# A hybrid decoder step on one core: the input projection by Strassen pairs, its forms made ahead of the recurrence, the pooling behind it

## The chip, the core and the metric

The kernel runs on one core of a Trainium2 chip. The core has a matmul engine (TensorE, PE in the profile, with PEld for its weight loads), VectorE (DVE), ScalarE (ACT), GpSimd (POOL) and an engine that issues DMAs (SyncE, SP). Each engine runs its own list of instructions in order and waits on semaphores for the others. The metric is the device time of one execution in microseconds (us); smaller is better.

## What is computed

One step of a one-layer decoder for 512 prompt tokens and 64 sample tokens, 576 columns in all, of 1024 features in float32:

```python
h = rms_norm(x, g_mix)
u, zq, zf, zi, zg, ga, gb = split(h @ w_in)            # 512 512 512 512 512 1024 1024 columns
pooled = multiscale_pool([state_pool; u]) - u          # windows 2, 4, 8, 16, one per group of 128
pool_out = einsum('btgc,gcd->btgd', pooled, w_pool_mix) * pool_scale
fg = lb + (1 - lb) * sigmoid(zf)
o, s_new = hgrn2_recurrence(silu(zq), 1 - fg, zi, log(fg), state)   # 4 heads, in chunks
o = o * rsqrt(mean(o * o) + eps) * hgrn_norm * silu(zg)
x = x + (sigmoid(ga) * (pool_out @ w_pool_up) + sigmoid(gb) * (o @ w_hgrn_up)) @ w_out
x = x + (silu(h2 @ w_ffn_gate) * (h2 @ w_ffn_up)) @ w_ffn_down      # h2 = rms_norm(x)
x = x + sigmoid(h3 @ w_ple_gate) * (p @ w_ple_proj)                 # h3 = rms_norm(x)
y = rms_norm(x, g_final)
```

The last 15 rows of u and the states of the recurrence are outputs too.

## The kernel before

Activations lie transposed: 128 features on the partitions, 576 tokens along the free dimension, in two halves of 288 (`H0`, `H1`). float32 products are made of two parts: every operand is split into a rounded high part and the rest, and a product is three matmuls, high by high, high by low and low by high.

A **unit** is 128 output features. In plain form (`mm`, L141) it takes 8 steps of 128 input features, 3 matmuls and 2 halves: 48 matmuls of 288 columns. Its weights come by one DMA of 512 KB into `raw`, and `split` makes `whi` on ACT (L78) and `wlo` on DVE (L79); with `src` given, `split_dma` has ACT write the negated weights (L87) and POOL issue a DMA that adds the weights to them in memory (L88). The list `seq` gives the order of the units, and `next_unit` loads and splits some units ahead.

A **Strassen pair** makes two units at once. Units by halves of tokens are a 2 x 2 product of blocks, and the Winograd form of Strassen's identity needs 7 block products in place of 8. Each is 4 steps x 3 matmuls = 12 matmuls of 288 columns, so a pair takes 84. On the side of the activations it needs seven **forms** per step: B11, B21 and B22 are the normed inputs, S1, S2, U3 and U4 are sums of them, all split in two parts (`form`, L811). On the side of the weights it needs sums of the two units' halves, each split again (A, B, C, D). Before the change the branch gates ga and gb and most of the feed-forward run by pairs (`pair`), with products software-pipelined over two sets of four PSUM banks; the first 20 units of the input projection run plain.

The stage around the change, in program order:

- Three units start with the loading of x, while the norm's sums are made. POOL adds some squares (L257). `rms` gives `rn`, the reciprocal norm (L285 on ACT, L286 on DVE), and `scaled` (L361) multiplies it into a unit's result.
- The units of `seq`: 0 to 3 are the pooling's input u, 8 to 11 f of the four heads, then by heads 16 (g), 4 (q), 12 (v), and so on. In PSUM `mm0` has four places of two banks, later `mm1` has two and `aux` four single banks.
- Pooling: `pool_in` (L385) scales u into a tile with the old state in front, `pool_vec` (L397) adds shifted copies and takes u off, `pool_mix` (L416) is the matmul per group. They are spread between the units.
- Recurrence per head: `forget` and `logf` (gate and its logarithm), `decays` (sums over chunks by scans and the factors by small POOL instructions, L443 to L478), `q_in` and `q_vec` (scaled q and k), `part1` (transposes and scores), `part2` (state updates, the tiny matmuls of L597), `part3` (output), `part4` (norm and gate), `part5` (split into `oh`, `ol`). Head h's parts stand between the units of head h + 1.
- Behind the heads come four pooled up units (`up_unit`, from `pho`), the last head's parts beside them, then four from the heads' outputs `oho`. The forms of the normed input are made beside these four (L815 to L822), then the pairs of ga and gb begin.

A scheduler of the language sets each engine's list from the program order and its own estimate of readiness; on the engine the list is fixed.

Of the kernel before, what the change touches and what calls it, by code (L numbers as in the profile page):

```python
# [28 lines left out]
def trunk(ctx: ExitStack, tc: tile.TileContext, a, o):  # L29
# [84 lines left out]
    state = {"raw": 0, "split": 0, "use": 0, "lim": out0, "pe": None}  # L114
    raws, splits = {}, {}

    def ahead(n_raw, n_split):
# [237 lines left out]
    def unit_mm(xs, pz=None):  # L355
        u = next_unit()
        pz = pz or ps_mm()
        mm(pz, u, xs)
        return pz

    def scaled(out, pz, rn):  # L361
        tt(out=v2(out), in0=pz[:, :, 0:HT], in1=v2(rn), op=MULT)  # L362
# [404 lines left out]

# [603 lines left out]
```

## Time and profile before

| what | value |
|---|---|
| median of 3 runs | 833.74 us (833.62 to 833.76) |
| profiled execution, first to last instruction | 831.3 us |
| PE busy | 820.8 us, 99% |
| DVE, ACT, POOL busy | 605.9, 505.0, 112.2 us |
| norm's matmuls end, fourth unit starts | 27.4 us |
| first pooled up unit starts | 182.3 us |
| first pair of ga starts | 237.1 us |

The profiled execution has no time of its own beside its span; the 2.4 us up to the median lie before the first and behind the last instruction. A row of instructions has its start and duration or, grouped, count, busy time and mean, then the idle time of the engine just before it with what ended it. L12 is line 12 of the kernel. Matmuls are pipelined: the spacing of their starts is their price, not their duration.

### The profile page before, as it was taken

Reading aid. Unit: us, or ns where it says so; the run is one execution under the profiler, and the core shown is the slowest. Engines: PE = TensorE matmul, PEld = TensorE weight load, DVE = VectorE, ACT = ScalarE, POOL = GpSimd, SP = SyncE. Lnnn points to the kernel's source line nnn. Section 1 sums busy time; section 2 is a strip of 40 time slices with the busy share of each in tenths; the row PEclk is TensorE's granted clock in tenths of the full one; section 3 lists DMA queues with packets and bytes.
Section 4 is the critical chain, followed back from the end, with each engine's and each line's share of the span. In section 5 each row is a group of like instructions: output and inputs, shape, how many; then the busy total and the mean of one; then the engine's idle time right before and its main releaser. Section 6 shows DMA issues by size and latency. Waiting matters only on the chain.

```text
span 831.3 us, 15196 instructions
## 1 busy us (share of the span) xinstructions
PE 820.8 (99%) x6092; PEld 807.0 (97%) x6092; DVE 605.9 (73%) x1008; ACT 505.0 (61%) x829; POOL 112.2 (13%) x194
## 2 busy tenths in 40 slices
PE   8999999999999999999999999999999999999996
PEld 7999999999999999999999999999999999999996
DVE  7977777764887776547978778777787767558846
ACT  7356436557777665446667767666676666645534
POOL 6204120000111110000111221112211121000000
PEclk9999999999999999999999999999999999999999
DMA  7421231222747674246866687657876668462103
GB/s 261 143 81 51 76 106 62 97 102 80 191 101 184 166 171 141 76 108 146 185 133 143 142 215 182 151 133 176 193 178 162 130 154 202 125 170 92 62 2 114
DMA packets 39046, 111.95 MB, mean 135 GB/s; under 512 B 4928, under 2 KB 9280, under 8 KB 38976
## 3 DMA queue, kind: packets, MB, share of 16 engines
q1 hardware_dynamic: 24288, 74.51, 26.8%
q0 software_dynamic: 12528, 33.30, 23.8%
q10 hardware_dynamic: 2160, 3.19, 1.0%
q8 instruction: 47, 0.77, 0.4%
q14 instruction: 23, 0.19, 0.1%
HBM read 105.98 MB, written 5.00 MB: 133 GB/s over the span
## 4 chain that ended last, share of the span: by engine, by line
PE 91%; DVE 3%; DMA 2%; ACT 2%; POOL 1%; issue 1%; SPq 0%; DVEq 0%
PE bb L877 7%; PE bb L876 7%; PE bb L878 7%; PE mm L155 5%; PE mm L153 5%; PE mm L157 5%; PE ba L878 4%; PE ba L877 4%; PE ba L876 4%; PE bd L878 2%; PE bd L877 2%; PE bd L876 2%; PE bc L877 2%; PE bc L876 2%; PE bc L878 2%; PE ba L157 2%
## 5 line engine op out<-in xcount | busy, mean ns | idle before, releaser
L78 ACT CAST whi<-raw 128x1024 fp32r<-128x1024 f32 (+2 forms) x50 | 46.8, 940 | 71.2 <-PE mm L155 36.6
L153 PE MATMUL mm<-hh,whi 128*128 128x288 f32 x320 | 70.6, 301 | 1.4 <-DVE ta L362 0.9
L155 PE MATMUL mm<-hl,whi 128*128 128x288 f32 x320 | 70.0, 298 | 0.4 <-DVE hl L246 0.3
L157 PE MATMUL mm<-hh,wlo 128*128 128x288 f32 x320 | 68.8, 296 | 0.0
L79 DVE TENSOR_TENSOR wlo<-raw,whi 128x1024 fp32r<-128x1024 f32 (+2 forms) x50 | 57.0, 1145 | 11.8 <-ACT whi L78 11.2
L87 ACT ACTIVATE wlo<-raw 128x1024 fp32r<-128x1024 f32 (+1 forms) x49 | 49.2, 1004 | 26.0 <-PE ba L878 17.6
L861 DVE TENSOR_TENSOR clo<-raw,chi 128x1024 fp32r<-128x1024 f32 (+1 forms) x38 | 43.3, 1139 | 27.3 <-ACT chi L857 27.3
L153 PEld LDWEIGHTS mm<-hh,whi 128*128 128x128 f32 x320 | 51.9, 189 | 4.2 <-ACT whi L78 1.6
L155 PEld LDWEIGHTS mm<-hl,whi 128*128 128x128 f32 x320 | 51.7, 189 | 1.4 <-DVE hl L246 1.0
L157 PEld LDWEIGHTS mm<-hh,wlo 128*128 128x128 f32 x320 | 51.5, 189 | 0.1
L861 DVE TENSOR_TENSOR wlo<-rb,whi 128x1024 fp32r<-128x1024 f32 (+1 forms) x38 | 43.3, 1139 | 11.2 <-ACT whi L857 10.9
L857 ACT CAST chi<-raw 128x1024 fp32r<-128x1024 f32 (+1 forms) x38 | 36.9, 972 | 9.8 <-DVE raw L853 9.8
L857 ACT CAST whi<-rb 128x1024 fp32r<-128x1024 f32 (+1 forms) x38 | 37.4, 983 | 6.4 <-PE bb L877 2.8
L87 ACT ACTIVATE dl<-rb 128x512 fp32r<-128x512 f32 (+1 forms) x38 | 22.7, 598 | 30.0 <-PE bc L878 28.1
L1010 ACT ACTIVATE bc<-bb 128x288 f32<-128x288 f32 x38 | 15.0, 395 | 41.1 <-PE bb L878 41.0
L91 ACT CAST whi<-raw 128x1024 fp32r<-128x1024 f32 (+1 forms) x37 | 35.9, 971 | 0.0
L847 DVE TENSOR_TENSOR rb<-rb 128x512 f32<-128x512 f32 (+1 forms) x38 | 24.6, 647 | 7.8 <-ACT dh L91 7.6
L886 DVE TENSOR_TENSOR cz<-bc,p 128x288 f32<-128x288 f32 x38 | 17.3, 456 | 14.8 <-PE bc L878 14.6
L883 DVE TENSOR_TENSOR cz<-bb,p 128x288 f32<-128x288 f32 x38 | 17.3, 456 | 14.2 <-PE bb L878 9.1
L852 DVE TENSOR_TENSOR raw<-raw,rb 128x512 f32<-128x512 f32 (+1 forms) x38 | 24.6, 647 | 1.2 <-ACT whi L91 0.5
L853 DVE TENSOR_TENSOR raw<-raw 128x512 f32<-128x512 f32 (+1 forms) x38 | 24.6, 647 | 0.8
L88 POOL DMA_DIRECT2D wlo<-in_w_ffn_gate x13 | 11.1, 855 | 103.5 <-ACT wlo L87 103.5
(789 smaller groups left out, 3228.0 us busy)
## 6 DMA issues: line engine op xcount, KB each, us to landing
raw<-in_w_in SPq DMA_DIRECT2D x25, 512.0 KB, 3.4
raw<-in_w_ffn_gate SPq DMA_DIRECT2D x13, 512.0 KB, 4.7
raw<-in_w_ffn_up SPq DMA_DIRECT2D x13, 512.0 KB, 5.0
wlo<-in_w_ffn_gate POOLq DMA_DIRECT2D x13, 512.0 KB, 5.6
wlo<-in_w_ffn_up POOLq DMA_DIRECT2D x13, 512.0 KB, 5.6
rb<-in_w_ffn_gate SPq DMA_DIRECT2D x9, 512.0 KB, 4.5
rb<-in_w_ffn_up SPq DMA_DIRECT2D x9, 512.0 KB, 5.0
raw<-in_w_dn SPq DMA_DIRECT2D x12, 384.0 KB, 3.8
```

What stands on the lines that cost most here:

```text
L78: nc.scalar.copy(out=hi[:, cs], in_=raw[:, cs])
L79: tt(out=lo[:, cs], in0=raw[:, cs], in1=hi[:, cs].bitcast(F32), op=SUB)
L87: neg = act(lo, raw, AF.Copy, scale=-1.0)
L91: nc.scalar.copy(out=hi, in_=raw)
L153: nc.tensor.matmul(out=out[h], lhsT=wh, rhs=xh[:, h * HT:(h + 1) * HT], start=first, stop=False)
L155: nc.tensor.matmul(out=out[h], lhsT=wh, rhs=xl[:, h * HT:(h + 1) * HT], start=False, stop=False)
L157: i = nc.tensor.matmul(out=out[h], lhsT=wl, rhs=xh[:, h * HT:(h + 1) * HT], start=False, stop=last)
L857: nc.scalar.copy(out=tiles[0][:, 0:2 * q["W"]], in_=q[raw][:, 0:2 * q["W"]])
L861: tt(out=lo, in0=q[raw][:, 0:2 * q["W"]], in1=hi.bitcast(F32), op=SUB)
L876: nc.tensor.matmul(out=out, lhsT=wh, rhs=xh, start=k == 0 and not seeded, stop=False, **kw)
L877: nc.tensor.matmul(out=out, lhsT=wh, rhs=xl, start=False, stop=False, **kw)
L878: i = nc.tensor.matmul(out=out, lhsT=wl, rhs=xh, start=False, stop=k == n - 1, **kw)
```

## The change

Of the 20 units, three f units run with the norm as before, and the fourth f, q and v of head 0 run plain behind it. The other 14 run as seven pairs, `in_pair`: g of heads 0 and 1, v with q of head 1, v with q of head 2, g of heads 2 and 3, v with q of head 3, and two pairs of u. Their forms `mforms` are made right behind the norm, with the reciprocal norm multiplied into the inputs; the sums in them (L794 to L797) are issued on POOL. The pairs of ga and gb use the same forms later. A pair of this stage runs in one set of four banks, its products one behind the other, with copies of bank contents on ACT between them. The inputs' tiles are then used for the recurrence, and x is loaded again for the residual. Units 11, 4 and 12 have their low weights made by `split_dma`. The pooling's additions and its mixing stand behind the recurrence, beside the up units of the heads' outputs, and the pooled up units come last.

```diff
-    seq = [W[m] for m in (0, 1, 2, 3, 8, 9, 10, 11, 16, 4, 12, 17, 5, 13, 18, 6, 14, 7, 15, 19)]
+    seq = [W[m] for m in (8, 9, 10, 11, 4, 12)]
...
-    seq += [up[i] for i in range(KD)]
+    seq += [up[i] for i in (4, 5, 6, 7, 0, 1, 2, 3)]
...
-            if plain0 <= i < dn0 or i in (dn0 + 1, dn0 + 2) or up0 + 4 <= i < out0 and i % 2:
+            if 3 <= i < up0 or plain0 <= i < dn0 or i in (dn0 + 1, dn0 + 2) or up0 + 4 <= i < out0 and i % 2:
                 kw["src"] = seq[i]
...
+    def split_form(tiles, src):
+        nc.scalar.copy(out=tiles[0], in_=src)
+        tt(out=tiles[1], in0=src, in1=tiles[0].bitcast(F32), op=SUB)
...
+    z = unit_mm(hx, [bank(t) for t in "cd"])
+    forget(3, z)
+    zq0 = unit_mm(hx, [bank(t) for t in "ab"])
+    zv0 = unit_mm(hx, [bank(t) for t in "cd"])
+    PIN = [("g", 0, 16, 17), ("vq", 1, 13, 5), ("vq", 2, 14, 6), ("g", 2, 18, 19), ("vq", 3, 15, 7), ("u", 0, 0, 1), ("u", 2, 2, 3)]
...
+    def i_sums(q):
+        ra, rb = q["ra"], q["rb"]
+        tt(out=rb[:, K1], in0=rb[:, K0], in1=rb[:, K1], op=ADD)
+        tt(out=rb[:, K0], in0=rb[:, K0], in1=ra[:, K0], op=SUB)
+        tt(out=ra[:, K0], in0=ra[:, K0], in1=rb[:, K1], op=SUB)
+        tt(out=ra[:, K1], in0=ra[:, K1], in1=ra[:, K0], op=ADD)
...
+    def in_pair(n):
...
+        i_load(n + 2)
+        za, zb, zc, zd = (bank(t) for t in "abcd")
+        i_prod(za, q, "A", 0, "B11", False)
+        act(zb, za, AF.Copy)
+        if nq:
+            i_ad(nq)
+        i_prod(zd, q, "B", 0, "S1", False)
+        p5 = fp.tile([P, HT], F32, name="p5", tag="p5", bufs=1)
+        nc.scalar.copy(out=p5, in_=zd)
+        i_prod(zb, q, "C0", 0, "S2", True)
+        act(zc, zb, AF.Copy)
+        if nq:
+            i_sums(nq)
+        i_prod(za, q, "A", 1, "B21", True)
...
+        i_prod(zb, q, "B", 1, "U3", True)
...
+            tt(out=cz[:, H1], in0=zb, in1=p5, op=ADD)
+        if nq:
+            i_b(nq)
+        i_prod(zc, q, "D", 0, "U4", True)
...
+        i_prod(zb, q, "C1", 0, "B22", True)
...
+    for k in range(4):
+        for j in (k, k + 4):
+            stt(out=res[j], in0=res[j], scalar=g_mix[:, j:j + 1], in1=rn, op0=MULT, op1=MULT)
+    for k in range(4):
...
+        pt_ = nc.gpsimd.tensor_tensor
+        pt_(out=ss[:, H0], in0=ha[:, H1], in1=hb[:, H1], op=SUB)
+        pt_(out=ss[:, H1], in0=ss[:, H0], in1=ha[:, H0], op=SUB)
+        pt_(out=uu[:, H0], in0=ha[:, H1], in1=ha[:, H0], op=SUB)
+        pt_(out=uu[:, H1], in0=hb[:, H0], in1=ss[:, H1], op=ADD)
+        fa, fb = form_tiles(HT, f"fa{k}"), form_tiles(T, f"fb{k}")
+        split_form(fa, ha[:, H0])
+        split_form(fb, hb)
+        fs, fu = form_tiles(T, f"fs{k}"), form_tiles(T, f"fu{k}")
+        split_form(fs, ss)
+        split_form(fu, uu)
+        store_forms(mforms, fa, fb, fs, fu)
+    with tc.issue_after(state["tanh"]):
+        for h in range(4):
+            logf(h)
+    i_load(0)
+    i_load(1)
+    q0 = pin[0]
+    i_ad(q0)
+    i_sums(q0)
+    i_b(q0)
...
     decays(0)
...
+    q_vec(0)
     decays(1)
...
+    in_pair(0)
+    part1(0)
+    in_pair(1)
+    part2(0)
...
+    in_pair(5)
+    part2(3)
+    part3(3)
+    in_pair(6)
+    part4(3)
+    part5(3)
...
+    for i in range(4):
+        up_unit(i, oho)
+        pool_mix(i, pool_vec(i))
...
-        form(i, g_mix, rn, mforms)
         if i == 2:
             first = p_all(0)
             next(first)
             next(first)
-        up_unit(i, oho, two_banks)
+        up_unit(i, pho)
...
     for n in range(*run):
+        res.append(pers.tile([P, T], F32, name="res", tag=f"res{n}"))
+        nc.sync.dma_start(out=res[n], in_=a["x"][n])
         pair(n)
```

Three places in the engines' lists. First PE, the first unit behind the norm's matmuls, before (`mm` is the PSUM place, `hh` and `hl` the input's parts, `whi` and `wlo` the weights'):

```order
L153 MATMUL mm<-hh,whi 128x288 [waits PE_49,Activation_49]
L153 MATMUL mm<-hh,whi 128x288
L155 MATMUL mm<-hl,whi 128x288 x2
L157 MATMUL mm<-hh,wlo 128x288 [waits DVE_49]
L157 MATMUL mm<-hh,wlo 128x288
```

and with the change (`bc` and `bd` are banks c and d):

```order
L153 MATMUL bc<-hh,whi 128x288 [waits DVE_49,Activation_49]
L153 MATMUL bd<-hh,whi 128x288
L155 MATMUL bc<-hl,whi 128x288
L155 MATMUL bd<-hl,whi 128x288
L157 MATMUL bc<-hh,wlo 128x288 [waits DMASW2_49]
L157 MATMUL bd<-hh,wlo 128x288
```

The unit's low weights come by a DMA of POOL's queue where DVE made them; four matmuls stand ahead of that wait.

Second DVE, behind the first scalings with the norm, before (`oscf` and `pf` are the pooling's tiles, `lbs` and `fc` the bounds of the decay):

```order
L683 TENSOR_TENSOR lbs<-lbe 128x4
L79 TENSOR_TENSOR wlo<-raw,whi 128x1024
L684 RECIPROCAL lbs<-lbs 128x4
L404 TENSOR_TENSOR oscf<-oscf 128x710
L685 TENSOR_TENSOR lbs<-lbs,lbe 128x4
L409 TENSOR_TENSOR oscf<-oscf,wc 128x2
L413 SCALAR_TENSOR_TENSOR pf<-oscf 128x64
L686 TENSOR_SCALAR fc_526<-lbs 128x4
L687 TENSOR_SCALAR fc_525<-lbs 128x4
L412 SCALAR_TENSOR_TENSOR pf<-oscf 128x512
```

and with the change (`res` are the scaled inputs, `fa` to `fu` with `l` the low parts of the forms, `ss` and `uu` POOL's sums, `gt` the last head's f):

```order
L787 SCALAR_TENSOR_TENSOR res3_81<-res3_81,C_76,rn_356 128x576
L787 SCALAR_TENSOR_TENSOR res7_85<-res7_85,C_76,rn_356 128x576
L375 TENSOR_TENSOR fa0l_621<-res0_78,fa0h_620 128x288
L375 TENSOR_TENSOR fb0l_623<-res4_82,fb0h_622 128x576
L375 TENSOR_TENSOR fs0l_629<-ss_614,fs0h_628 128x576
L375 TENSOR_TENSOR fu0l_631<-uu_615,fu0h_630 128x576
L360 TENSOR_TENSOR gt_501<-bc_439,rn_356 128x288
L360 TENSOR_TENSOR gt_501<-bd_440,rn_356 128x288
L375 TENSOR_TENSOR fa1l_643<-res1_79,fa1h_642 128x288
L375 TENSOR_TENSOR fb1l_645<-res5_83,fb1h_644 128x576
```

The pooling's steps are gone from here, and the reading of banks c and d stands behind the eight scaled inputs and the first set of forms.

Third ACT, at the same stage, before (`whi` of the next units, `nps` the pooling's output rows, `gt` and `kt` of the first head):

```order
L682 ACTIVATE lbe_523<-lbe_523 128x8
L78 CAST whi_455<-raw_445 128x1024
L395 DMA out_new_pool<-nps_427 128x135
L78 CAST whi_540<-raw_447 128x1024
L395 DMA out_new_pool<-nps_434 128x135
L395 DMA out_new_pool<-nps_441 128x135
L395 DMA out_new_pool<-nps_511 128x135
L78 CAST whi_599<-raw_449 128x1024
L431 ACTIVATE gt_593<-gt_593 128x576
```

and with the change, where the forms end and the first pair's weights begin (`raw_710` and `rb_712` are that pair's weights, `wlo_719` and `whi_718` its A):

```order
L374 CAST fs3h_694<-ss_680 128x576
L374 CAST fu3h_696<-uu_681 128x576
L389 ACT_TABLE_LOAD
L389 ACTIVATE lt_702<-gt_417 128x576
L389 ACTIVATE lt_704<-gt_422 128x576
L389 ACTIVATE lt_706<-gt_427 128x576
L389 ACTIVATE lt_708<-gt_501 128x576
L87 ACTIVATE wlo_719<-raw_710 128x1024
L91 CAST whi_718<-raw_710 128x1024
L78 CAST whi_732<-rb_712 128x1024
```

The negated copy of the first pair's A weights stands behind the casts of all forms, a table load and the four logarithms.

More of the change, by code (lines that the diff above doesn't have):

```diff
@@ L416, in pool_mix, with halves @@
-    def pool_mix(g):
-        qh, ql = pho[g]
-        for h in range(2):
-            sl = slice(h * HT, (h + 1) * HT)
-            px = ps_aux()[:, 0:HT]
-            nc.tensor.matmul(out=px, lhsT=wpm[:, g * P:(g + 1) * P], rhs=pooled[g][:, sl], start=True, stop=True)
-            act(qh[:, sl], px, AF.Copy, scale=pscale[:, g:g + 1])
-            stt(out=ql[:, sl], in0=px, scalar=pscale[:, g:g + 1], in1=qh[:, sl].bitcast(F32), op0=MULT, op1=SUB)
+    def halves(z):
+        return list(zip((H0, H1), z))
@@ L623, in part3 @@
         act(sq, ot, AF.Square)
[L624 removed]
+        s["sq"] = [pers.tile([P, T], F32R, name="sqr", tag=t) for t in ("hh4", "hh5")]
         nc.scalar.copy(out=s["sq"][0], in_=sq)
@@ new lines, in i_prod @@
+    def i_prod(out, q, u, second, name, seeded):
+        hi, lo = q[u]
+        kw = {"skip_group_check": True} if seeded else {}
+        for k in range(4):
+            wh, wl = (w[:, second * 512 + k * P:second * 512 + (k + 1) * P] for w in (hi, lo))
+            xh, xl = mforms[name][k]
+            nc.tensor.matmul(out=out, lhsT=wh, rhs=xh, start=k == 0 and not seeded, stop=False, **kw)
+            nc.tensor.matmul(out=out, lhsT=wh, rhs=xl, start=False, stop=False, **kw)
+            nc.tensor.matmul(out=out, lhsT=wl, rhs=xh, start=False, stop=k == 3, **kw)
@@ L732, in trunk @@
-    g_vec(3, unit_mm(hx))
+    in_pair(0)
+    part1(0)
+    in_pair(1)
+    part2(0)
+    q_vec(1)
+    part3(0)
+    part1(1)
+    decays(2)
+    part4(0)
+    part5(0)
+    in_pair(2)
+    part2(1)
+    q_vec(2)
+    part3(1)
+    part1(2)
+    decays(3)
+    part4(1)
+    part5(1)
+    in_pair(3)
+    part2(2)
+    part3(2)
+    in_pair(4)
+    q_vec(3)
+    part1(3)
+    part4(2)
+    part5(2)
+    in_pair(5)
[4 more added lines that the diff above has]
+    part5(3)
+    with tc.issue_after(state["exp"]):
+        act(actw, eps, AF.Tanh)
@@ L736, in trunk, with pool_mix @@
+    def pool_mix(g, pf):
+        qh, ql = pho[g]
+        for h in range(2):
+            sl = slice(h * HT, (h + 1) * HT)
+            px = ps_aux()[:, 0:HT]
+            nc.tensor.matmul(out=px, lhsT=wpm[:, g * P:(g + 1) * P], rhs=pf[:, sl], start=True, stop=True)
+            act(qh[:, sl], px, AF.Copy, scale=pscale[:, g:g + 1])
+            stt(out=ql[:, sl], in0=px, scalar=pscale[:, g:g + 1], in1=qh[:, sl].bitcast(F32), op0=MULT, op1=SUB)
     pab = [[], []]
-    def up_unit(i, xs, banks=None):
+    state["lim"] = out0
```

343 lines of the change are left out of this document (181 added, 162 removed).

## The prediction

> **What bounds the kernel now.** I read the page's engine table and chain first, then who makes TensorE (PE) wait, then PE by stage.
>
> ```profile
> span 831.3 us, 15196 instructions
> PE 820.8 (99%) x6092; PEld 807.0 (97%) x6092; DVE 605.9 (73%) x1008; ACT 505.0 (61%) x829; POOL 112.2 (13%) x194
> PE 91%; DVE 3%; DMA 2%; ACT 2%; POOL 1%; issue 1%; SPq 0%; DVEq 0%
> PE mm L153 <- DVE ta L362: 0.9, 1, 0.9
> 27.40:182.30 154.90, 154.01 (x1121) 145.77 (x1122) 115.37 (x221) 81.19 (x144) 22.18 (x64) 1.00 0.27 89
> ```
>
> PE is busy 99% of the span and makes 91% of the chain. The fourth row, of the table of waits, is the only wait of PE in the stage that the change rewrites: 0.9 us. The last row is that stage (length, then busy time of PE, weight loads, VectorE (DVE), ScalarE (ACT) and GpSimd (POOL)): the input projection from the fourth unit on, with the recurrence and the pooling. PE lacks 0.9 of 154.9 us, while DVE works 115.4 and ACT 81.2 beside it. So the kernel ends when PE has done its matmuls, and a change gains what it takes from them and loses what it makes PE wait.
>
> **Fewer matmuls.** A matmul's price is the spacing of starts. First a plain unit, then a Strassen product as the later stages already run it:
>
> ```profile
> 28.04 0.43 PE L157 MATMUL mm<-hh,wlo 128*128 128x288 f32 x2
> 35.76 0.43 PE L155 MATMUL mm<-hl,whi 128*128 128x288 f32 x2
> 249.98 0.30 PE L876 MATMUL bb<-fs0h,chi 128*128 128x288 f32 x1
> 257.02 0.29 PE L878 MATMUL ba<-fa1h,wlo 128*128 128x288 f32 x1
> ```
>
> Between the first two rows lie 58 matmuls, 7.72 / 58 = 0.133 us each; between the last two 53, 7.04 / 53 = 0.133. Fourteen plain units are 14 x 48 = 672 matmuls, seven pairs 7 x 84 = 588: 84 fewer, **-11.2 us**. The projections up, the mixing and the recurrence keep their matmuls. The old 0.9 us wait is on a step that is rebuilt: **-0.9**.
>
> **The forms, on the path.** Before, the forms were made beside the up projections, under a full PE. Now they stand between the norm and the first pair, and PE has only three plain units to do meanwhile (last head's f, first head's q and v): 144 x 0.133 = 19.2 us from 27.4. What DVE has to do in that time, by these rows:
>
> ```profile
> L286 DVE RECIPROCAL rn<-rn 128x288 f32<-128x288 f32 x2 | 3.8, 1920 | 0.0
> L815 DVE SCALAR_TENSOR_TENSOR clo<-res,C,rn 128x576 f32<-128x576 f32 x4 | 3.3, 814 | 0.7 <-PE bb L157 0.7
> L809 DVE TENSOR_TENSOR fb0l<-clo,fb0h 128x576 fp32r<-128x576 f32 x1 | 0.8, 752 | 0.0
> L809 DVE TENSOR_TENSOR fa0l<-chi,fa0h 128x288 fp32r<-128x288 f32 x1 | 0.5, 459 | 0.9 <-ACT fa0h L808 0.9
> L852 DVE TENSOR_TENSOR raw<-raw,rb 128x512 f32<-128x512 f32 x1 | 0.7, 686 | 0.0
> L79 DVE TENSOR_TENSOR wlo<-raw,whi 128x1024 fp32r<-128x1024 f32 x23 | 28.1, 1228 | 6.8 <-ACT whi L78 6.7
> L448 DVE TENSOR_TENSOR_SCAN gt<-cmask,lt 128x576 f32<-128x576 f32 x4 | 5.3, 1346 | 2.0 <-ACT lt L437 2.0
> 42.65 0.75 DVE L362 TENSOR_TENSOR gt<-mm,rn 128x576 f32<-128x576 f32 x1
> 43.32 0.89 DVE L404 TENSOR_TENSOR oscf<-oscf 128x708 f32<-128x708 f32 x1
> ```
>
> The last two rows show that a 0.75 us instruction is followed after 0.67, so I take 0.08 off each. DVE starts the reciprocals at about 27.0 and ends them at 30.8. Three f heads by halves (six of 0.36) with small ones of the decay bounds: 2.6. Eight scaled inputs at 0.73: 5.8. Low parts of four sets of forms, each 0.38 + 3 x 0.67: 9.6. The last f head: 0.7. That ends at 49.5. Behind it stand the sums, split and scalings of the first pair and of q and v (four sums 0.6 each, one low part 1.15, two of 0.6, four halves 0.37: 6.2) and, up to the addition that frees bank b for the pair's last product, two and a half heads of decays (three scans of 1.26) and the first head's q work: 13.1. By this queue alone the last product of pair 0 could start at about 69.
>
> The sums inside the forms go to POOL, 16 of 288 columns. The nearest rows are POOL's additions of 576, with what DVE did meanwhile; the first row is such a DVE instruction undisturbed:
>
> ```profile
> 7.14 0.42 DVE L79 TENSOR_TENSOR wlo<-raw,whi 128x256 fp32r<-128x256 f32 x1 [0.55 <-ACT whi L78]
> 8.97 1.49 POOL L257 TENSOR_TENSOR ssum<-ssum,sq 128x576 f32<-128x576 f32 x1 [7.18 <-ACT sq L256]
> 9.22 1.52 DVE L79 TENSOR_TENSOR wlo<-raw,whi 128x256 fp32r<-128x256 f32 x1
> 20.50 1.42 POOL L257 TENSOR_TENSOR ssum<-ssum,sq 128x576 f32<-128x576 f32 x1
> 20.36 2.17 DVE L316 TENSOR_TENSOR ssum<-ssum,sq 128x576 f32<-128x576 f32 x1
> ```
>
> The DVE instruction of 0.42 us took 1.52 and ended at 10.74, just its own time after POOL's end at 10.46; the addition of 576 columns, 0.75 elsewhere, took 2.17 and ended 0.6 after POOL's. While POOL adds, DVE stands still. So POOL's work is added to DVE's: half of 1.42 is 0.72 for 288 columns, 16 x 0.72 = 11.5. Bounds: 0 (POOL runs only where DVE waits anyway) and 16 x 1.5 = 24 (no cheaper for half the columns); I take 11.5, since the columns are half and the rows are of this very operation.
>
> PE against this queue, step by step.
> (a) Units 11, 4 and 12 now get their low weights by a negated copy on ACT and an accumulating DMA from POOL, not by DVE.
>
> ```profile
> L87 ACT ACTIVATE wlo<-raw 128x1024 fp32r<-128x1024 f32 x3 | 3.2, 1061 | 0.0
> L437 ACT ACT_TABLE_LOAD x1 | 1.3, 1283 | 0.0
> L437 ACT ACTIVATE lt<-gt 128x576 f32<-128x576 f32 x4 | 2.4, 674 | 0.0
> wlo<-in_w_in POOLq DMA_DIRECT2D x7, 512.0 KB, 5.5
> ```
>
> The copy of unit 11 can end at 26.5 (ACT casts until 25.4, then 1.06), the DMA lands 5.5 later, at 32.0. PE starts the unit at 27.4 and needs the low part after four matmuls, at 27.9: **4 us** of standing; everything of PE is queued behind. The f unit ends at about 37.7, q's at 44.
> (b) v's unit takes the banks of the last f head, which DVE reads only behind the eight inputs, the first set of forms and some ten POOL additions: 33.4 + 5.8 + 2.4 + 7.2 + 0.7, at 49.5. PE waits **5.5 us**; the unit ends at 55.9.
> (c) Pair 0's first product needs its A weights. On ACT their copy stands behind all form casts, a table load and four logarithms. The last sums of POOL end near 56, the cast behind them at 57, table and logarithms at 61 (the last waits for the last input's reader on DVE), the copy at 62, the DMA lands at 67.3. PE does two matmuls meanwhile: **11 us**.
> (d) From 67 on DVE has 13.1 us and some waits for ACT and POOL's decay factors ahead of the addition after product U3: about 82; the last product then ends at 84.5. PE's own work from 27.4 to there is 19.2 + 11.2 and the first head's transposes and scores, 4.7 by these rows (5.3 less four foreign matmuls):
>
> ```profile
> 168.92 0.60 PE L542 MATMUL aux<-ident,ta 128*128 128x128 f32 x4
> 173.94 0.33 PE L572 MATMUL aux<-qk 128*64 128x64 f32 x2
> ```
>
> That is 35.1, so without waits it would end at 62.5. The loss of (a) to (d) together is 84.5 - 62.5 = **+22.0**; the parts overlap a little and are not added again. Without POOL's hold on DVE, (c)'s chain lands at 57.5 and DVE's queue passes at 70 to 72, with 12.5 lost: the lower bound. With 24 us of POOL it is 34.
>
> **Pairs 1 to 6.** Each pair costs DVE four sums, one split of 1024 and two of 512 where two units cost two splits of 1024: 4 x 0.6 + 1.15 + 1.2 against 2.3, 2.5 us more, and ACT some 4.5 (copies of banks, two negated copies). Less the pooling, which leaves this stage, their lists come by the rows' durations to some 88 us of DVE and 76 of ACT, under 104 us of PE (6 x 11.2 and three and a half heads of recurrence). Followed by hand through pairs 1 and 2, every seed copy and addition is there before PE wants it, though with 1 us to spare at places, and each waits in line behind splits of 1 us on one buffered bank set. I take **+1.5** for six pairs; bounds 0 (PE showed 0.9 of wait in the old stage) and 12 (two late evictions of 1 us in each pair).
>
> **The tail.** The last head's norm and gate now have no pooled up projection to stand under. PE finishes pair 6, does the norm's matmuls, then 36 of the first up unit (three heads, both halves) = 4.8 us, then needs the last head. In the old trace that chain was:
>
> ```profile
> 198.38 0.30 PE L634 MATMUL aux<-sqr,onesv 128*128 128x288 f32 x1
> 202.59 0.62 ACT L750 COPY pab<-mm 128x576 f32<-128x576 f32 x1
> 206.35 1.05 ACT L86 CAST whi<-raw 128x1024 fp32r<-128x1024 f32 x1
> 207.30 1.06 ACT L87 ACTIVATE wlo<-raw 128x1024 fp32r<-128x1024 f32 x1
> 208.26 0.66 ACT L651 CAST oh<-ot 128x576 fp32r<-128x576 f32 x1
> ```
>
> From 198.4 to 208.9 are 10.5 us; the copy for the up unit (0.6) and part of the casts for the next weights (1.7) are foreign: 8.2. Less 0.5 of the norm's own matmuls and 4.8 of cover: 2.9, and 0.4 for the low part: **+3.3** (2 to 5.5). Behind it four up units (25.5 us) cover DVE's work there, about 20 (ten pooling additions like the 0.89 above, four steps of 512, eight halves, five splits of 1.15). The eight reloads of x, the state of the pool in four loads and the mixing weights ride on queues that are half empty: no cost; a late mixing weight would cost 2.
>
> **Sum.** 831.3 - 11.2 - 0.9 + 22.0 + 1.5 + 3.3 = 846.0 for the span. What lies around it is 833.74 - 831.3 = 2.4 for the median of three runs, so **848.4 us**. A measurement of this kernel tells about 0.2% (1.7 us) from no change.
>
> **The clock.** Granted clock (the column after PE's count) around the tiny state matmuls:
>
> ```profile
> 182.00:183.00 1.00, 1.00 (x6) 0.62 0.71 102
> 183.00:184.00 1.00, 1.00 (x6) 0.50 0.88 344
> 185.00:186.00 1.00, 1.00 (x7) 0.67 0.00 0
> ```
>
> Once in this stage it is halved for 3.4 us, which costs 1.7; I leave that as it is. [...]
>
> **Rivals.**
> 1. POOL does not hold DVE back here: it would run in DVE's waits for ACT's casts. Against it the two pairs of rows above. Loss 12.5 instead of 22: 839. Chance 0.15.
> 2. The pairs themselves are bound by DVE and ACT: lines of 1 us instructions ahead of each bank's eviction. For it the single set of banks and DVE at 85%; against it the hand count. +10: 858. Chance 0.15.
> 3. [...] Chance 0.08. [...]
> 4. Faster: POOL works beside DVE, and ACT gets pair 0's weight copy out before the logarithms would let it, so that the low part lands near 52 and PE's three units cover most of the forms. Up to the first pair 6 us are then lost instead of 22, and 831.3 - 12.1 + 6 + 3.3 + 2.4 = 831. It decides where all waits together stay under 10.4 us (12.1 less 1.7). Against it: the copy stands behind the logarithms in ACT's fixed list. Chance 0.07.
>
> **Numbers.** The forecast with its own bounds (843 to 853) has 0.55. The range takes in rivals 1 to 3 and most of the pairs' bound: 837 to 860; rival 4 and a worse rival 2 stay out, 0.12 together. Faster by over 0.2% is rival 4: 0.07; within 0.2% the lower edge of rival 1: 0.04; slower 0.89.
>
> **What would show it.** Waits of PE: on the DMA of the first unit (4 us), on a DVE reading of bank c (5.5), on the DMA of pair 0's A weights (4) and the cast before (7), in the tail on the cast of the last head (3). DVE's instructions beside POOL's 288-column additions would take about 0.7 longer. Wrong would be DVE at its usual durations there, PE without a gap of 5 us before pair 0, or waits of over 1 us in every later pair.

## The result, and the profile after

| | before | after |
|---|---|---|
| time, median of 4 runs | 833.68 us (831.4 to 833.76) | 862.01 us (860.64 to 866.69) |
| ratio | | 1.0364 (95%: 1.0329 to 1.0399) |
| profiled execution: span | 831.3 us | 859.4 us |
| TensorE busy, and the rest of the span | 820.8, 10.5 | 820.8, 38.6 |

The kernel became 28 us slower; 848.4 was forecast, with 860 as the upper end. The direction was right, the size was not. One profiled execution below, that of gap_fill, was granted 0.19 of the clock in the mean and took 4069 us; only its waits up to the end of pair 0 are read from it. First the page after: the span, the engines, the chain, and TensorE's granted clock in 40 slices of 21.5 us.

```profile
span 859.4 us, 15207 instructions
PE 820.8 (96%) x6008; PEld 805.2 (94%) x6008; DVE 616.4 (72%) x1026; ACT 540.6 (63%) x908; POOL 144.1 (17%) x223
PE 85%; ACT 3%; issue 2%; POOL 2%; DVE 2%; DVEq 0%; ACTq 0%; POOLq 0%
PEclk9787999999999999999999999999999999999999
```

TensorE issues 84 matmuls fewer (6008 for 6092) and yet is busy for the same 820.8 us: what the matmuls gave, 11.2 us, has gone into slower ones. The clock row shows the larger part of it, in slices 2 to 4. And TensorE stands 28.1 us longer. Who made it wait (time, occasions, longest):

```profile
PE ba L690 <- ACT whi L91: 8.1, 1, 8.1
PE bc L153 <- DVE gt L360: 5.9, 1, 5.9
PE ba L692 <- DMA wlo<-in_w_in: 3.9, 1, 3.9
PE bc L153 <- ACT oh L604: 3.9, 1, 3.9
PE bc L153 <- DVE plo L894: 1.6, 1, 1.6
PE bb L690 <- ACT bb L725: 1.4, 1, 1.4
PE aux L500 <- DVE kS L472: 1.4, 1, 1.4
PE bb L690 <- DVE u L752: 1.3, 1, 1.3
PE aux L524 <- ACT vn L497: 1.0, 1, 1.0
PE bc L157 <- DMA wlo<-in_w_in: 0.8, 1, 0.8
PE ba L690 <- DVE sg L745: 0.5, 1, 0.5
```

Rows 2 and 10 are the f unit, rows 1 and 3 pair 0's A weights, rows 7 and 9 the first head's transposes and scores, rows 6, 8 and 11 the later pairs, rows 4 and 5 the tail. Then the clock: the six stretches in which it was halved (length, busy time of PE, weight loads, DVE, ACT and POOL, then the granted clock).

```profile
29.37:39.61 10.24, 5.93 (x23) 5.61 (x24) 9.89 (x20) 6.54 (x9) 3.42 (x3) 0.50 0.94 235
60.09:73.74 13.65, 5.78 (x23) 5.42 (x24) 10.29 (x16) 11.14 (x16) 6.58 (x12) 0.50 0.48 118
104.46:107.87 3.41, 3.41 (x17) 3.41 (x16) 3.05 (x10) 1.84 (x4) 1.47 (x9) 0.50 0.89 225
128.35:131.77 3.42, 3.42 (x17) 3.42 (x16) 3.42 (x6) 1.63 (x4) 0.00 (x0) 0.50 0.20 46
189.80:193.21 3.41, 3.41 (x16) 3.41 (x15) 1.81 (x6) 0.40 (x1) 0.00 (x0) 0.50 0.78 281
213.69:217.10 3.41, 3.41 (x15) 3.34 (x15) 2.93 (x10) 1.96 (x5) 0.00 (x0) 0.50 0.34 91
```

Half of the busy time in them is lost: 25.36 / 2 = 12.7 us, where the trace before had one dip of 1.7. So 11.0 us more, and the account closes: -11.2 for the matmuls, +11.0 for the clock and 28.1 more idle time make 27.9 of the measured 28.1. This is an account of TensorE's time, not yet of causes: the first dip's 3.0 us stand ahead of the wait for pair 0, which full clock there would only have made longer (f_bank below). Rows 1 and 2 lie in the gaps ahead of the f unit and of pair 0, the last behind the wait of the tail. Rows 3 to 5 follow three of the four state updates, where TensorE never stopped. This is what it issued ahead of the fourth row, and the first matmul in it that shows the half speed by its 0.44 for 0.30:

```profile
125.18 0.43 PE L548 MATMUL aux<-As,vk 64*128 64x64 f32 x2
125.54 1.95 PE L550 MATMUL aux<-lt,S 128*128 128x8 f32 x16
127.35 0.48 PE L557 MATMUL aux<-vb,t 96*128 96x512 f32 x1
128.20 0.30 PE L691 MATMUL ba<-fa1l,whi 128*128 128x288 f32 x1
128.53 0.44 PE L690 MATMUL ba<-fa2h,whi 128*128 128x288 f32 x1
```

Last, DVE, GpSimd and ACT at the end of the forms:

```profile
55.71 1.35 DVE L375 TENSOR_TENSOR fb3l<-res,fb3h 128x576 fp32r<-128x576 f32 x1
58.44 0.76 DVE L375 TENSOR_TENSOR fu3l<-uu,fu3h 128x576 fp32r<-128x576 f32 x1
```

```profile
56.40 1.30 POOL L797 TENSOR_TENSOR uu<-res,ss 128x288 f32<-128x288 f32 x1
```

```profile
62.03 1.04 ACT L87 ACTIVATE wlo<-raw 128x1024 fp32r<-128x1024 f32 x1
```

The same low part of 576 columns takes 1.35 us beside GpSimd's sums and 0.76 behind them; the copy for pair 0's A weights ends at 63.1, where 62 was forecast.

### The profile page after: what moved, and what is told of

It reads as the page before. It is cut to its first block, busy times and chain, and to the rows that moved or that the text cites. A ratio compares the mean times of both kernels' runs of the same rounds, so it can differ in the third digit from the quotient of the medians.

```text
span 859.4 us, 15207 instructions
## 1 busy us (share of the span) xinstructions
PE 820.8 (96%) x6008; PEld 805.2 (94%) x6008; DVE 616.4 (72%) x1026; ACT 540.6 (63%) x908; POOL 144.1 (17%) x223
## 3 DMA queue, kind: packets, MB, share of 16 engines
q0 software_dynamic: 14976, 40.38, 27.9%
## 4 chain that ended last, share of the span: by engine, by line
PE 85%; ACT 3%; issue 2%; POOL 2%; DVE 2%; DVEq 0%; ACTq 0%; POOLq 0%
PE bb L1008 6%; PE bb L1009 6%; PE bb L1007 6%; PE ba L1009 4%; PE ba L1008 4%; PE ba L1007 4%; PE bd L1009 2%; PE bd L1008 2%; PE bd L1007 2%; PE bc L1008 2%; PE bc L1009 2%; PE bc L1007 2%; PE bc L153 2%; PE bc L155 2%; PE bd L153 2%; PE bd L155 2%
## 5 line engine op out<-in xcount | busy, mean ns | idle before, releaser
L87 ACT ACTIVATE wlo<-raw 128x1024 fp32r<-128x1024 f32 (+1 forms) x59 | 59.8, 1013 | 25.0 <-PE ba L1009 19.2
L992 DVE TENSOR_TENSOR clo<-raw,chi 128x1024 fp32r<-128x1024 f32 (+1 forms) x38 | 43.3, 1139 | 28.5 <-ACT chi L988 28.5
L78 ACT CAST whi<-raw 128x1024 fp32r<-128x1024 f32 (+2 forms) x33 | 29.1, 888 | 28.5 <-PE bd L155 14.3
L79 DVE TENSOR_TENSOR wlo<-raw,whi 128x1024 fp32r<-128x1024 f32 (+2 forms) x33 | 36.1, 1100 | 12.7 <-ACT whi L78 12.2
L91 ACT CAST whi<-raw 128x1024 fp32r<-128x1024 f32 (+1 forms) x44 | 43.2, 982 | 0.0
L988 ACT CAST chi<-raw 128x1024 fp32r<-128x1024 f32 (+1 forms) x38 | 36.9, 972 | 8.6 <-DVE raw L984 8.6
L1017 DVE TENSOR_TENSOR cz<-bc,p 128x288 f32<-128x288 f32 x38 | 17.3, 454 | 14.8 <-PE bc L1009 14.7
L86 ACT CAST whi<-raw 128x1024 fp32r<-128x1024 f32 x15 | 15.7, 1047 | 18.4 <-PE bb L155 9.5
L88 POOL DMA_DIRECT2D dl<-in_w_in x15 | 13.0, 867 | 81.5 <-ACT dl L87 77.6
L88 POOL DMA_DIRECT2D wlo<-in_w_in x17 | 14.5, 852 | 72.5 <-ACT wlo L87 49.9
L91 ACT CAST dh<-rb 128x512 fp32r<-128x512 f32 (+1 forms) x45 | 26.0, 577 | 0.0
L979 DVE TENSOR_TENSOR rb<-rb,raw 128x512 f32<-128x512 f32 (+1 forms) x38 | 24.4, 643 | 0.4
L88 POOL DMA_DIRECT2D wlo<-in_w_dn x14 | 11.9, 847 | 65.7 <-ACT wlo L87 49.4
```

What stands on the lines that cost most here:

```text
L78: nc.scalar.copy(out=hi[:, cs], in_=raw[:, cs])
L79: tt(out=lo[:, cs], in0=raw[:, cs], in1=hi[:, cs].bitcast(F32), op=SUB)
L87: neg = act(lo, raw, AF.Copy, scale=-1.0)
L88: nc.gpsimd.dma_start(out=lo, in_=src, accum_op=ADD)
L91: nc.scalar.copy(out=hi, in_=raw)
L988: nc.scalar.copy(out=tiles[0][:, 0:2 * q["W"]], in_=q[raw][:, 0:2 * q["W"]])
```

## The experiments

Theory going in: the loss is work without cover (the forms, ahead of the first pair) plus half clock (12.7 us in the trace after), which the author took to follow stretches in which TensorE moves few columns. Rivals: GpSimd's hold on DVE is the loss; one list (ACT's) is the loss; the pairs themselves are too slow. All times below are medians beside runs of the kernel before on the same chip; "idle" is span less TensorE's busy time (10.5 us before, 38.6 after), "clock" the loss as worked out above (1.7 and 12.7).

| run | median us | ratio to before (95%) | idle | clock |
|---|---|---|---|---|
| fill_state | 863.61 | 1.0372 (1.0344 to 1.0401) | 37.7 | 7.2 |
| spread | 862.59 | 1.0357 (1.0332 to 1.0382) | 41.2 | 10.8 |
| before_again | 833.25 | 0.9996 (0.9980 to 1.0012) | 10.0 | 0.0 |
| gap_fill | 881.74 | 1.0587 (1.0557 to 1.0618) | - | - |
| a_first | 864.12 | 1.0382 (1.0352 to 1.0411) | 40.3 | 12.6 |
| dve_sums | 855.16 | 1.0285 (1.0251 to 1.0320) | 31.9 | 11.3 |
| f_bank | 867.39 | 1.0411 (1.0375 to 1.0448) | 43.9 | 13.8 |
| one_set | 853.71 | 1.0235 (1.0201 to 1.0270) | 32.2 | 13.1 |
| joint | 852.52 | 1.0232 (1.0206 to 1.0257) | 30.2 | 13.5 |
| tail | 858.96 | 1.0316 (1.0274 to 1.0357) | 36.9 | 15.8 |
| cover | 856.61 | 1.0284 (1.0259 to 1.0308) | 36.7 | 9.4 |
| cover_first | 847.65 | 1.0181 (1.0147 to 1.0216) | 24.3 | 11.3 |
| cover_lists | 853.10 | 1.0245 (1.0218 to 1.0272) | 28.5 | 14.7 |

### The clock

**fill_state**, wide matmuls among the small ones of the state update:

```diff
             nc.tensor.matmul(out=py[:, b * 8:(b + 1) * 8], lhsT=S0[:, b], rhs=qb[:, TP + b * 8:TP + (b + 1) * 8], start=False, stop=b == 7)
+            if b in (1, 3, 5, 7):
+                filler(3)
```

> Twelve matmuls of 288 columns on old operands are put among the sixteen of 8 columns in the state update of each head, three behind every second pair: 48 x 0.133 = 6.4 us more work. Theory 1 (the clock falls to half where a stretch of about 3.4 us holds hardly any moving columns, as these sixteen of 8 columns over 1.95 us with small ones around them, though TensorE counts as busy): the dips at 104, 128 and 190 are gone, 1.7 us each, and the span grows by 6.4 - 5.1 = 1.3. Theory 2 (the dips have another cause): they stay and the span grows by 6.4.

```profile
104.00:135.00 31.00, 31.00 (x232) 29.24 (x232) 24.82 (x58) 21.83 (x46) 5.77 (x19) 1.00 0.40 112
186.00:196.00 10.00, 10.00 (x79) 9.67 (x78) 6.14 (x16) 2.12 (x7) 1.11 (x4) 1.00 0.54 165
```

The clock is whole where it was halved three times, its loss falls by 5.5 us, and 6.4 us of added work cost 1.6 in the median, as theory 1 has it (1.3). One trace could have missed the dips by its place on the clock's grid (before_again, below); but the four executions were granted 0.978 to 0.984 of the clock, the four of the change 0.970 to 0.977.

**spread**, nothing added, only the order:

```diff
+    def state_mm(h):                        # the lines of part2, with a yield behind each matmul
...
             nc.tensor.matmul(out=out, lhsT=wl, rhs=xh, start=False, stop=k == 3, **kw)
+            next(tiny[0], None)
...
+    tiny[0] = state_mm(0)
     in_pair(1)
```

> The state's matmuls of 8 columns are issued among the products of the pair ahead of their head's update, one step between groups of three products, instead of in one row with the update; the same matmuls, nothing added. Theory 1 (a stretch of about 3.4 us with hardly any moving columns is what halves the clock at 104, 128 and 190): two or three of these dips are gone and the span falls by 3 to 5 us. Theory 2 (the dips have another cause, and the 48 wide matmuls of the earlier run only moved them): they stay, and the span changes by less than 1.

Only heads 0 and 3 came apart. For heads 1 and 2 the old state arrives late, and the sixteen still stand in a row. The first two rows are of head 0, the others of heads 1 and 2:

```profile
90.36 0.39 PE L540 MATMUL aux<-lt,S 128*128 128x8 f32 x2
90.82 0.28 PE L540 MATMUL aux<-lt,S 128*128 128x8 f32 x2
120.13 1.95 PE L540 MATMUL aux<-lt,S 128*128 128x8 f32 x16
147.39 1.85 PE L540 MATMUL aux<-lt,S 128*128 128x8 f32 x16
```

Dips began at 122.2 and 149.5, right behind the two rows, and at none of the other two updates. So the dips went with the unbroken row, as theory 1 has it, though on one case only: head 3's update began at a place of the grid where every update in one row was followed by a dip, head 0's at one where none was (both below). The time did not fall, since 2.6 us of new waiting ate what one dip less gave.

**before_again**, the kernel before without an edit.

> The kernel before, unchanged, for a second profile of its clock. Theory 1 (the clock looks at stretches of 3.413 us on a grid that lies differently in each execution, and halves itself for the next one behind a stretch with few moving columns): the dip is not at 182 again but at one to three of the four state updates, by where the grid falls, each 1.7 us. Theory 2 (the dip belongs to a place of the program): one dip at 182.

```profile
span 829.5 us, 15196 instructions
```

```profile
27.00:230.00 203.00, 201.93 (x1485) 193.41 (x1484) 148.44 (x279) 116.01 (x206) 25.93 (x68) 1.00 0.32 99
```

No dip at all this time, and the span is 1.8 us shorter, the price of the one before. Theory 2 falls (the dip does not belong to 182); theory 1's "one to three" was one too many. In the eight traces with seven pairs the updates without fillers were followed by two or three dips, before by one and by none. In these traces it goes by where a row of sixteen falls on the grid of the dips (3.413 us, last section). Beside the row at 125.54 shown above, the trace after has these:

```profile
102.06 1.95 PE L550 MATMUL aux<-lt,S 128*128 128x8 f32 x16
147.39 1.95 PE L550 MATMUL aux<-lt,S 128*128 128x8 f32 x16
187.04 1.95 PE L550 MATMUL aux<-lt,S 128*128 128x8 f32 x16
```

Their stretches of the grid begin at 101.05, 124.94, 145.42 and 186.38 us, so the four rows begin 1.01, 0.60, 1.97 and 0.66 us into them. Only the third runs over the end of its stretch, and only it has no dip behind it. In before_again the four begin at 0.13, 2.92, 2.79 and 2.46 us. The thirteen traces without fillers hold 47 such unbroken rows: all 25 that begin 0.35 to 1.58 us into a stretch are followed by a dip at its end (one of them runs over it by 0.12), and none of the 22 that begin earlier or later. So the number of these dips goes by the place of the grid and not by the row, which is the same in both kernels. Why the grid lay so in most of the changed kernels (2.06 to 2.70 us behind the start of the span, modulo 3.413, in seven of the eight traces) is not settled.

**gap_fill**, 120 matmuls whose result nobody reads ahead of pair 0:

> 120 matmuls of 288 columns on old operands into a spare bank stand on TensorE between v's unit (ends at 56) and pair 0; nothing waits for them, and at 0.133 us they end at 72, where the weights of pair 0 have landed. Theory 1 (an idle TensorE is given half the clock, and keeps it 3 us into the work): the dip from 60 to 73.6 goes, 2.9 us of lost work with it, and the span falls by 2 to 3. Theory 2 (the half clock there is not a matter of idling): the dip stays and the span is within 1 us of the changed kernel's.

Neither came, but +20 us. With the filler the engines' lists came out otherwise: the copy that seeds pair 0's bank b stood behind both heads' decays on ACT, and TensorE waited 17.1 us for it. The question was answered by the kernels with cover, below.

### The forms' stage

**a_first**, pair 0's A weights ahead of the forms:

```diff
+    i_load(0); i_load(1); q0 = pin[0]; i_ad(q0)
     for k in range(4):
...
+    i_sums(q0); i_b(q0); i_c(q0, 0); i_c(q0, 1)
     with tc.issue_after(state["tanh"]):
...
-    i_load(0); i_load(1); q0 = pin[0]; i_ad(q0)
-    i_sums(q0); i_b(q0); i_c(q0, 0); i_c(q0, 1)
```

> Pair 0's two loads and the copy, cast and accumulating transfer of its A weights stand ahead of the forms on ACT, and the four logarithms behind the rest of its weights. Theory 1 (the place of these weights in ACT's list sets when the pairs can start; in the changed kernel TensorE waited 8.1 us on their cast and 3.9 on their transfer, until 72.7): both waits go; the first product starts when v's unit ends, at about 56, the next one waits for DVE's sums and split of the B weights behind the last form (59.2 + 2.4 + 1.2, so about 63), and the span falls by 8 to 10 us. Theory 2 (the recorded step (d): DVE's queue holds the last product of pair 0 to about 84 whatever ACT does): the wait only moves to a DVE operation inside pair 0 and the span falls by less than 2.

```profile
PE bb L690 <- ACT bc L732: 7.7, 1, 7.7
PE bc L153 <- DVE gt L360: 6.5, 1, 6.5
PE ba L690 <- DVE ta L360: 4.3, 1, 4.3
```

```profile
78.75 0.26 ACT L427 ACTIVATE fac<-fac 128x68 f32<-128x68 f32 x1 [3.63 <-POOL fac L419]
79.48 0.39 ACT L732 ACTIVATE bc<-bb 128x288 f32<-128x288 f32 x1
```

The two waits went (that on the transfer had ended at 68.8 us, not at the 72.7 of the expectation) and others of the same size came, in two places: DVE's reading of q's bank a stands behind its forms (4.3), and the seed copy of bank c stands on ACT behind the second head's exponential, which itself waits 3.6 us for GpSimd's decay factors (7.7). The time is as theory 2 says, the place is not: it was ACT's list again.

**dve_sums**, `pt_ = tt` in place of GpSimd's `tensor_tensor`.

> The sixteen sums inside the forms go to DVE instead of GpSimd. Theory 1 (GpSimd and DVE exclude each other, so that GpSimd's sums, 20 us from first to last, only stretch DVE's list): DVE does the sums in 16 x 0.38 = 6.1 us, its form lows fall from 1.2 to 0.75 each, the last form is ready 3 us earlier than 59.2, and the span falls by 2 to 4. Theory 2 (GpSimd's sums run beside DVE and take 6 us off it): the forms come 3 to 6 us later and the span grows by as much.

-6.9 us in the median: theory 1's direction, but hardly by its mechanism. The low parts took 10.8 us in all in place of 17.5, the sums took as much back, and the last low part ended only 0.4 us earlier (58.8). Nearly all the rest is the new lists: the copy for the A weights now stood ahead of the logarithms, and where after had 8.1 and 3.9, the trace shows

```profile
PE ba L690 <- DVE ta L360: 4.5, 1, 4.5
PE bb L690 <- ACT bc L732: 1.8, 1, 1.8
```

**f_bank**, the f unit in banks that nobody holds, and DVE's splits for units 11, 4 and 12:

```diff
+    z = ps_mm()                            # before close("mm0")
+    u = next_unit(); mm(z, u, hx)
+    forget(3, [z[:, i, 0:HT] for i in range(2)])
-    z = unit_mm(hx, [bank(t) for t in "cd"])
-            if 3 <= i < up0 or plain0 <= i < dn0 or ...
+            if plain0 <= i < dn0 or ...
```

> The last head's f unit goes to the fourth pair of banks of the first pool, which nothing holds, and units 11, 4 and 12 get their low weights from DVE again instead of by an accumulating transfer. TensorE's waits of 5.9 us (on DVE reading the banks) and 0.8 us (on the transfer) in front of this unit go. Theory 1 (pair 0's start is set by ACT's and DVE's lists, so that waits ahead of it cost nothing by themselves): the three units end 6 us earlier and TensorE waits that much longer for pair 0; the span falls by less than 2, or grows by up to 3 with DVE's three splits. Theory 2 (each wait of the account adds to the time): the span falls by 6 to 7.

```profile
PE ba L692 <- ACT whi L91: 15.2, 1, 15.2
PE ba L694 <- DMA wlo<-in_w_in: 3.3, 1, 3.3
```

```profile
26.00:41.00 15.00, 13.89 (x102) 13.49 (x101) 14.71 (x23) 11.51 (x18) 3.41 (x4) 1.00 0.53 142
```

As theory 1 has it, 18.5 us of waiting now stand in one place, where 18.7 stood in four (5.9 + 0.8 + 8.1 + 3.9). The window row shows the other half: without the gap the three units run at full clock, where after was at 0.50 from 29.4 to 39.6. So the half clock there came with the gap of 5.9 us, and neither that dip nor the f unit's wait cost anything by itself, as long as pair 0 could not start: its weights were there at 67.5 us, and at 68.8 in the trace after. By the ratios the kernel even lost 4 us more, 1 above what theory 1 allowed for DVE's three splits. In the trace the loss lies behind pair 0's start, in a wait of 2.2 us and three stretches of half clock from 84.1 on (5.1 us); whether the splits brought them is not shown.

**one_set**, a quarter of the forms' work:

```diff
-    for k in range(4):
+    for k in range(1):
...
-        store_forms(mforms, fa, fb, fs, fu)
+        for _ in range(4):
+            store_forms(mforms, fa, fb, fs, fu)
```

> Only the first of the four sets of forms is made and used four times over; the sums, casts and low parts of the other three are left out (12 sums on GpSimd, 12 casts on ACT, 12 low parts on DVE), so the output is not the reference's. Everything else stands. This prices the forms where they stand. Theory 1 (the loss is the forms, ahead of the first pair and without cover, with the half clock behind the gap): the forms are ready at 46, long before v's unit ends; the waits on pair 0's weights (8.1 + 3.9 us) and the dip from 60 to 73 (2.9) go, the wait of the f unit shrinks, and the span falls by 14 to 20 us, to 840 to 845. What is then left over the kernel before, 9 to 14 us with 11.2 us of matmuls saved, is the pairs, the clock's other dips and the tail. Theory 2 (the pairs themselves are what is too slow): the waits come back inside pairs 0 and 1, and the span falls by less than 8.

Only -8.3 us by the medians, 10.7 by the ratios, between the two theories. Pair 0 began as soon as v's unit was done, and then stood 4.2 us for DVE's reading of v's banks, which the list had put behind the first pair's splits and part of the decays, and the clock was halved from 60.7 to 70.9 all the same. Three quarters of the forms are worth 8 to 11 us; 20 us of loss remain without them.

**joint**, most of it at once with seven pairs: a_first, dve_sums, tail, the reads of q's and v's banks ahead of the forms, and

```diff
-        act(zb, za, AF.Copy)
+        with tc.high_priority():
+            act(zb, za, AF.Copy)           # the same for zc and p5
-        nc.scalar.dma_start(out=o["new_pool"][g], in_=nps)
+        nc.gpsimd.dma_start(out=o["new_pool"][g], in_=nps)
```

> Five edits at once on the changed kernel, all seven pairs kept: the forms' sums on DVE, pair 0's A weights ahead of the forms, the reads of q's and v's banks ahead of the forms, the copies that seed a pair's banks and that of the shared product ahead of the decays' exponentials on ACT, the last norm ahead of the last pair, the pool's state written out from GpSimd's queue. Theory 1 (each single edit only moved the wait to the next list in line, and together they take the whole of it): TensorE waits only for the forms themselves, from 56 to about 60, the waits of 7.7 and 4.3 us of the earlier run do not come back, and the span is 843 to 848. Theory 2 (DVE's list as a whole sets it): DVE still has its 20 us for the forms and 13 for decays and q ahead of pair 0's last additions, and the span stays above 850.

852.5: theory 2's side of the line, by waits of 1.8, 2.1 and 2.3 us at three places inside pair 0 and three single dips between 60 and 78. The f unit kept its banks, and its waits of 6.4 and 1.2 us are still there; since TensorE no longer stood ahead of pair 0, they now count. Seven pairs with f_bank's edit as well were not run; the kernels with cover have it.

### The tail, and cover

**tail**:

```diff
-    in_pair(6)
     part4(3)
     part5(3)
+    in_pair(6)
```

> The last head's norm and gate (part4 and part5 of head 3) are written ahead of the last pair instead of behind it. Theory 1 (the tail's 3.9 us, TensorE waiting for the cast of the last head, is a chain without cover, and the clock's dip at 213 follows from that wait): the pair covers the chain, the wait on the cast and the dip go, and the span falls by 3.9 + 1.7 = 5 to 6 us. Theory 2 (the chain is bound by the length of ACT's and DVE's lists, not by its place): the wait stays over 2.5 us or a new one of that size stands in front of the last pair, and the span changes by less than 2.

The wait on the last head's cast and the dip at 213 went, but small waits took back 2.2 us of 3.9. By the ratios the kernel gained some 4 us; its profiled execution happened to have another three stretches of half clock from 84 on, right behind pair 0, where after had none.

**cover**, two units plain among the forms, six pairs, the first one for the pooling branch:

```diff
-    seq = [W[m] for m in (8, 9, 10, 11, 4, 12)]
+    seq = [W[m] for m in (8, 9, 10, 11, 4, 12, 16, 17)]
-PIN = [("g", 0, 16, 17), ("vq", 1, 13, 5), ("vq", 2, 14, 6), ("g", 2, 18, 19), ("vq", 3, 15, 7), ("u", 0, 0, 1), ("u", 2, 2, 3)]
+PIN = [("u", 0, 0, 1), ("vq", 1, 13, 5), ("vq", 2, 14, 6), ("vq", 3, 15, 7), ("g", 2, 18, 19), ("u", 2, 2, 3)]
```

> Units 16 and 17 go plain again, among the forms, and the first pair that uses forms is one of the pooling branch, which the recurrence does not wait for; the sums of the forms are on DVE, the f unit is in the free banks, the last norm is written ahead of the last pair. Six pairs instead of seven: 72 matmuls less than before instead of 84, 1.6 us given back. Theory 1 (the loss is the missing cover over the forms, and the half clock that follows the gap): the waits ahead of the first pair fall from 19 us to under 3, the dip behind them goes, and with -9.6 for the matmuls, 5 us of waits in the pairs and 2 in the tail the kernel comes to 829 to 836. Theory 2 (the pairs themselves are too slow beside the recurrence): the waits come back inside the pairs and the kernel stays above 845.

856.6 is on theory 2's side of the line, but not for its reason alone. The gaps ahead of the first pair shrank to 1.3, 2.8 and 0.2 us and 7.9 us of waits stood in the pairs (3.9, 2.4, 1.6), but 12.0 us appeared in the tail: ACT, which issued the pool's state to memory, stood twice for GpSimd's copies of it (2.8 and 3.1 us) with the last head's norm behind. **cover_first** changed what this trace showed:

> The kernel with units 16 and 17 plain among the forms, with the faults that its trace showed mended: the copies that seed a pair's banks ahead of the decays' exponentials on ACT (it waited 3.5 us), unit 4 split on DVE (2.8 us), the pool's state written out from GpSimd's queue instead of ACT's (ACT stood 5.9 us in the tail), the last head's values ahead of the norm before. Theory 1 (what is left is waits at named places): 8 to 12 us of waits go and with them two dips; the kernel comes to 838 to 846. Beating the kernel before (833) needs waits and dips together under 10 us. Theory 2 (the lists of ACT and DVE are full): the waits move on and it stays above 850.

```profile
26.00:75.50 49.50, 44.91 (x327) 43.43 (x325) 46.10 (x84) 42.66 (x63) 12.76 (x24) 1.00 0.59 139
```

```profile
PE ba L711 <- DMA wlo<-in_w_in: 5.9, 1, 5.9
PE bb L153 <- ACT u L789: 3.9, 1, 3.9
PE bd L153 <- DVE plo L914: 1.9, 1, 1.9
```

The first row is the stage that had the two gaps: full clock throughout (the next dip begins at 75.5, in the first of the waits below it, which ends at 79.0). This is the fastest variant, 14 us better than the change, and still slower than before, 1.0181 (1.0147 to 1.0216). Three waits and six dips are left. **cover_lists** put the work behind the three waits ahead on its engines:

> The covered kernel (847.7) with what its trace showed put ahead in the lists: the accumulating transfer of a pair's A weights ahead of the decay factors on GpSimd (TensorE waited 5.9 us), the last copies out of the pooling pair's banks ahead of the norms' logarithms on ACT (3.9 us), the mixing of each pool as soon as its vector is there (1.9 us). Theory 1 (each of these waits is on TensorE's path, since nothing behind the forms waits elsewhere any more): the three go, 11.7 us, with the two dips of the clock behind them 1.7 to 3 more, and the kernel comes to 833 to 837; what then keeps it from being faster than before by its 72 matmuls is the clock around the state updates. Theory 2 (the lists are full): at least half of the waits comes back elsewhere and it stays above 841.

Theory 2: the three went and others came, on the cast of the last head and on DVE and ACT in places that had been clean, and the kernel is 5 us slower than the last one:

```profile
PE bc L153 <- ACT oh L604: 6.3, 2, 3.6
PE bb L709 <- DVE cz L778: 3.2, 1, 3.2
PE aux L557 <- DVE vb L554: 2.6, 1, 2.6
```

No version beat the kernel before.

## Why the prediction was wrong

By its own sum: 846.0 was forecast for the span and 859.4 came, 13.4 more. In TensorE's account, 11.2 of these are in its busy time (the forecast had it fall by 11.2; it stayed) and 2.2 in its idle time (25.9 forecast: 26.8 less the old 0.9; 28.1 measured). By place the split is another one: pair 0 ended 5.4 us late (89.9 for 84.5), 2.5 of it by half clock; the dips behind it cost 6.8 us where the forecast left the old 1.7, so 5.1; pairs 1 to 6 and the tail took 2.1 and 2.2 more; and 1.1 us of small waits of the kernel before went. Together that is 13.7.

- **The clock is the step that failed**: "Once in this stage it is halved for 3.4 us, which costs 1.7; I leave that as it is." It was halved six times for 12.7, and 7.6 us of the surplus (2.5 + 5.1) are half clock. Half clock behind a gap had a chance of 0.08 (rival 3), and no run at hand showed it then. The trace after does: the dip behind the first wait, (a), vanished in the wait that followed, and those behind pair 0's gap and the tail's wait cost 2.5 and 1.7. What no part of the prediction has is that the dip behind a state update, there once, can come three times. The gaps' dips came with the change: cover_first shows the first two to end with the gaps, f_bank the first, tail the third. How many updates are hit goes by the place of the grid, as the kernel before shows with one dip and with none; why that place was so often a bad one in the changed kernels stays open.
- **Fewer matmuls**: right, 84, and eaten by the above.
- **(a)** 4 us forecast, 6.7 measured, with another cause. The f unit did not wait for its weights but for DVE to read the banks of an earlier head, out of which its own were cut; only 0.8 was the transfer. With the 3.0 of half clock behind it that makes 9.7, where (a) and (b) together had 9.5: v's unit ended at 56.0, 55.9 was forecast, and that was luck.
- **(b)** 5.5 forecast, none came: the units before ran late and the first of them at half clock, and DVE was through by then. f_bank shows that a wait which goes in (a) comes back in (c).
- **(c)** 11 forecast, 12.0 measured, by the chain named: casts, table, logarithms, copy (62 forecast, 63.1), transfer.
- **(d)** the last product of pair 0 was to end at 84.5 by DVE's list and ended at 89.9 (the row below the list). Behind the weights, which landed 1.5 us later than forecast (68.8), TensorE lost 2.5 to half clock and 2.4 to two waits in the first head's transposes and scores, where the forecast had 1.6 for DVE's list. a_first and joint show that ACT's list is as close behind as DVE's.
- **GpSimd's hold on DVE**: right in kind (1.35 for 0.76), so rival 1 fell. Its size was off: the sixteen sums took 20.0 us, not 11.5, and they held DVE up for less, since its sixteen low parts took 17.5 us where they took 10.8 in dve_sums, 6.7 more. What that is worth in the span could not be told from dve_sums, which changed the lists as well.
- **Pairs 1 to 6**: +1.5 forecast, 3.6 measured (0.5 + 1.4 + 1.3 and 0.4 for a copy of v). Rival 2 fell.
- **The tail**: +3.3 forecast, 3.9 and 1.6 measured. The 1.6, a low part of the pool's mixing, was counted as covered.

The end of pair 0's last product in the trace after, for (d):

```profile
89.61 0.30 PE L692 MATMUL bb<-fb3h,cl 128*128 128x288 f32 x1
```

## What to carry to other kernels

In a kernel whose TensorE is full, work that needs a result from the vector engines must not be put where TensorE has nothing else to do: a saving of 11 us in matmuls met 28 us of standing. Where several in-order lists end close together, taking away one wait shows the next list; price the stage by the time its last result is ready, not by the sum of waits. And count the clock: waits of 2.1 and 2.3 us in joint and three of the four rows of sixteen matmuls of 8 columns in the trace after were each followed by 3.41 us at half clock, 1.7 us of work; a wait of 2.3 us in spread was not, and the dip behind wait (a) was swallowed by the wait for pair 0.

## What the runs showed of the hardware

The dips lie on a grid. In the trace after they begin at 29.37, 60.09, 104.46, 128.35, 189.80 and 213.69 us, whole multiples of 3.413 us apart (44.37 = 13 x 3.413, 109.23 = 32 x 3.413), and last 3, 4, 1, 1, 1 and 1 of them; in the eleven other traces with more than one dip (those of the table without gap_fill and before_again) the dips keep the same grid with another offset. The first two and the last lie at waits of TensorE of 5.9, 8.1 and 3.9 us. The other three follow stretches in which TensorE counted as busy throughout, and in which a row of sixteen matmuls of 8 columns (1.95 us) began 1.01, 0.60 and 0.66 us from the start. In the traces without fillers such a row was followed by a dip where it began 0.35 to 1.58 us into a stretch (25 of 25 rows; none of 22 others). That the number of columns moved is what the clock goes by was the author's reading; it was not shown.

GpSimd's additions of 288 columns took 0.80 to 1.35 us (the first 2.31) beside DVE's low parts, nearly what 576 columns took before (1.42 and 1.49).
